# A list scheduler's table of durations: new figures for all engines, short strided copies, powers, selects and function table changes

## The chip, the cores and the metric

The kernel runs on one core of one Trainium2 chip. The metric is the device time of one execution in microseconds. The core's engines each work through a queue of their own and meet at semaphores: TensorE (PE in the profile; its weight loads are PEld), VectorE (DVE), ScalarE (ACT), GpSimd (POOL) and SyncE (SP), which here does nothing but issue all the DMAs.

## The reference

One encoder block on 1024 tokens by 1024 features, all in float32. Cut to what is computed:

```
h = rms_norm(x, g_mix);  proj = h @ w_in        # 8224 columns: glu a, b | q k v | z | logits | gates A, B
c = silu(layer_norm(depthwise_conv31(glu_a * sigmoid(glu_b))));  y_conv = c @ w_conv_out
q, k, v = silu(depthwise_conv5(q, k, v));  q, k = l2_norm(q), l2_norm(k)
o = gated_delta_rule(q, k, v, g, beta) + reversed(gated_delta_rule(reversed ...))   # 8 heads of 128
y_delta = (rms_norm(o) * silu(z)) @ w_delta_out
x = x + (sigmoid(gate_a) * y_conv + sigmoid(gate_b) * y_delta) @ w_o
x = x + (silu(gt) * up) @ w_down                 # gt, up = rms_norm(x) @ w_gate_up, 2816 columns each
x = x + sigmoid(rms_norm(x) @ w_pl_gate) * rms_norm(p @ w_pl_proj)
out = rms_norm(x)
```

The gated delta rule is a recurrence over chunks of tokens. In each chunk a triangular system is solved, and a 128x128 state goes from chunk to chunk, in both directions.

## The kernel before

**What is computed in which form.** Activations stand as [feature, token]. A dense product multiplies 128 columns of a weight with 512 tokens; operands are split into a high and a low part of a reduced float32 type (`split`: a cast on ACT and a subtraction on DVE), and three matmuls of 128x512 make one product block (`mm3`). In the profile these are the rows `ps<-big,w`. The delta rule works in plain float32 with matmuls of 128x128; each of those leaves two records in the profile, so eight records are four matmuls.

**The stages.** Part 1 begins with the start: eight loads of x, RMSNorm, transposes on PE with `ident`, x itself transposed and stored (`d<-mid`), and the taps of the convolutions (`in_qkv_conv_w`, `in_conv_dw_w`). Then come the input projections (`qkv`, `glu`, `z`, `gate`), the convolutions on DVE, the projection of the per-layer embedding (`pl`), the convolution's LayerNorm (`ln`) and projection (`cout`), and beside them the delta rule, in four groups of two heads. Part 3 is dense products throughout: delta's projection, the output projection, SwiGLU up and down, the per-layer embedding's gate, and the output.

**A head of the delta rule**, by the sections named in the code: `d.np` makes the matrices from q and k. `d.inv` inverts 32x32 diagonal blocks on DVE. `d.lev` puts them together to 128x128 inverses, twice for four chunks each: sixteen copies of 32 partitions on ACT bring the blocks to their places (`eu`, `et`: rows `COPY big<-big 32x4x32`, 32x128 in the profile), a product on PE, its negation on ACT (`m<-ps`), a second product, four more copies and two small transposes on DVE, then a third product, a negation, a fourth product and two copies. `d.chain` runs through the chunks, both directions in turn; each step is a product, a combination on DVE or ACT, and the next product (tiles `S`, `xin`, `z`). `d.out` adds the products within the chunks (matmuls `ps<-big,m`; two selects on POOL make the masks), takes squares with a sum on ACT (`m,sso<-big`), raises them to the power -1/2 on POOL (`rn`), multiplies on DVE (`m<-big,rn`) and transposes on PE (`ps<-ident,m`).

**What sets the order.** The block is first written down as a list of instructions on stand-ins for tiles (`add` and what calls it). `Plan.order` then gives them an order by list scheduling: each engine takes, at the time at which it comes free in the plan, the instruction of the lowest level that is ready by then; levels (`LV`) put weights first (-3.0), then the delta rule (-1.8), with the dense products behind (0.5 to 2.7). An instruction is ready when what it reads has ended in the plan, plus a latency by the two engines (`LAT`), and when its tiles have a free buffer. `HOLD` lets DVE wait up to 0.24 us for something more urgent; ACT passes over an instruction that needs another function table up to `AGE` = 4 times. The durations in the plan are the costs that `matmul`, `transpose`, `act`, `_vec`, `square_transpose`, `recip`, `pow`, `fill` and `select` write down, and `SWITCH` for a change of ACT's table; DMAs take `DMA_LAT` and a rate. The plan's times are used for nothing but the order: on the chip each engine runs its queue in that order, and the waits are real ones.

Of the kernel before, what the change touches and what calls it, by code (L numbers as in the profile page):

```python
# ---------------------------------------------------------------- the order of the instructions
# The block is first written down as a list of instructions on stand-ins for tiles. `Plan.run` gives
# them an order by list scheduling (which engine does what when, with what each instruction waits for
# and how many buffers there are) and then issues them in that order, on tiles made as they come up.
# [12 lines left out]
ALU = mybir.AluOpType  # L17
# [19 lines left out]
class Buf:  # L37
    """A stand-in for a tile."""
# [15 lines left out]
class View:  # L54
    """Part of a tile: partitions [p0, p1), free dimensions as (stride, size) from an offset."""
# [40 lines left out]
    def fold(self, *sizes):  # L96
        """The last free dimension cut into dimensions of these sizes."""
        s, n = self.dims[-1]
        dims = []
        for k in reversed(sizes):  # L100
            dims.append((s, k))
            s *= k
        return View(self.buf, self.p0, self.p1, self.off, self.dims[:-1] + dims[::-1], self.cast)
# [4 lines left out]
    def spread(self, *shape):  # L108
        """Dimensions of size one repeated to these sizes."""
# [28 lines left out]
class Op:  # L138
    """An instruction: its engine, how to issue it, and what it reads and writes."""


# functions that need a table of their own in ScalarE, and the price of a change of tables
TABLES = {AF.Exp: 0, AF.Sigmoid: 1, AF.Silu: 2, AF.Ln: 3}
SWITCH = 2.0
AGE = 4
# a DMA: from its issue to its data, and bytes in a microsecond
# [3 lines left out]
# from the end of an instruction to the start of one that needs it, by the engines of both  # L150
# [7 lines left out]
class VPool:  # L158
# [5 lines left out]
    def tile(self, shape, dtype=F32, tag=None, bufs=None, line=None, cap=99, stream=None):  # L164
        """line: tiles of a line are given out in the order of the program, at most cap at a time."""
# [7 lines left out]
class Plan:  # L173
# [11 lines left out]
    # -- recording  # L185
# [44 lines left out]
    # -- engines  # L230
    def matmul(self, out, lhsT, rhs, start, stop):
        n = rhs.n
        if rhs.buf.dtype == F32R and rhs.cast is None:
            cost = max(0.107, n / 2400 + 0.003)
        else:
            cost = 2 * max(0.107, n / 1200)
# [4 lines left out]
    def transpose(self, out, in_, ident):  # L241
        self.add("pe", lambda: self.nc.tensor.transpose(out.ap(), in_.ap(), ident.ap()), [out], [in_, ident], 0.107)  # L242

    def act(self, out, in_, func=AF.Copy, scale=1.0, bias=None, accum=None):
# [8 lines left out]
        if accum is not None:  # L253
            outs.append(accum)
            cost += 0.1
# [46 lines left out]
    def square_transpose(self, out, in_):  # L302
        self._vec("transpose", "dve", dict(out=out, in_=in_))

# [4 lines left out]
    def pow(self, out, in0, in1):  # L309
        self.add("pool", lambda: self.nc.gpsimd.tensor_tensor(out=out.ap(), in0=in0.ap(), in1=in1.ap(), op=ALU.pow),  # L310
                 [out], [in0, in1], 0.3 + out.n * 0.165)
# [5 lines left out]
    def select(self, out, in_, pattern, base, mult, op, fill=0.0):  # L317
        self.add("pool", lambda: self.nc.gpsimd.affine_select(
            out=out.ap(), in_=in_.ap(), pattern=pattern, base=base, channel_multiplier=mult, compare_op=op, fill=fill),
            [out], [in_], 0.14 + out.n * 0.00084)  # L320
# [13 lines left out]
    # -- scheduling  # L334
    def order(self):
# [6 lines left out]
        free_slots = {}     # (pool, tag) -> times at which slots come free  # L342
        queue = {}          # line -> tiles in program order
# [8 lines left out]
        wait = {e: [] for e in engs}       # heap by ready time: dependencies all scheduled  # L352
        avail = {e: [] for e in engs}      # heap by key: ready at the engine's time
# [6 lines left out]
        held = []                            # of a later phase  # L360
        last_end = {}
        parked = {}                          # (pool, tag) -> ops that wait for a slot
# [10 lines left out]
        def slots_ready(o, now):  # L373
            """None when it can go now; else (time or None, (pool, tag))."""
# [20 lines left out]
        while len(done) < total:  # L395
# [43 lines left out]
            # worth the wait: something more urgent is about to be ready  # L439
# [14 lines left out]
            o.start = now  # L454
            if o.table is not None and o.table != table:
# [46 lines left out]
    # -- issue  # L502
# [28 lines left out]
P = 128  # L531
# [25 lines left out]
# slots of each kind of tile, and what goes before what  # L557
# [22 lines left out]
# products of part 1 in order (k, q, v, g: glu, z, l: logits, p: per-layer embedding; with the head or  # L580
# block), and those that fill in
# [6 lines left out]
def ORDER(f):  # L588
    """The block up to the delta rule's end, in the order in which it is written down."""
# [10 lines left out]
def hybrid_block(tc, x, p, g_mix, w_in, conv_dw_w, conv_dw_b,  # L600
# [7 lines left out]
    big = pn.pool("big", N_BIG)          # 1024 columns and the padding of a convolution  # L608
    mid = pn.pool("mid", N_MID)          # 512 columns
# [30 lines left out]
    # ---------------------------------------------------------------- constants  # L640
# [13 lines left out]
    m_le = tri("m_le", 1, -1, 0, ALU.is_ge)      # 1 where partition <= column  # L654
    m_ge = tri("m_ge", -1, 1, 0, ALU.is_ge)      # 1 where partition >= column
    m_lt = tri("m_lt", 1, -1, 0, ALU.is_gt)      # 1 where partition < column
    m_gt = tri("m_gt", -1, 1, 0, ALU.is_gt)      # 1 where partition > column
    ident2 = const("ident2", [64, 32])           # two identities of 32, one above the other
# [18 lines left out]
    # ---------------------------------------------------------------- dense products  # L677
    def split(hi, lo, src, scale=None):
        """src (float32) as the sum of two float32r parts."""
# [7 lines left out]
    def load_w(w, r0, nk, c0, cap=4, pool=None):  # L687
        """nk blocks of 128 rows of w, 128 columns, split: by four blocks."""
# [22 lines left out]
    def block_half(w, acts, h, nk):  # L711
        """128 columns of w against 512 tokens: a bank of [column, token]."""
# [18 lines left out]
    def rows(r, n):  # L731
        """[P, n] values by token as a bank whose rows all hold them along the free axis."""
# [1033 lines left out]
```

## Time and profile before

| | us |
|---|---|
| median of 3 runs | 2144.21 |
| lowest, highest run | 2142.52, 2147.73 |
| profiled execution, span from first to last instruction | 2144.9 |
| PE busy in it | 2094.7 |
| DVE busy | 1606.4 |
| ACT busy | 1089.8 |
| POOL busy | 129.5 |

The page gives the profiled execution's span; its own time is not given beside it, and the span lies between the lowest and the highest of the runs. In the profile, a group's row has its line, engine, operation, tiles, shapes and count, then busy time and the mean of one in ns, then the idle time of the engine just before such instructions and what ended it. In the timeline a row has its start, its length, and in brackets the idle time before it. L242 and L237 are the lines of the transpose and of the matmul, L259 and L266 those of ACT, L282 of DVE, L310, L314 and L318 of POOL, L330 of the DMAs.

### The profile page before, as it was taken

The page shows a single profiled execution, that of the slowest core. Times are in us where ns is not written, and L with a number is a line of the kernel's source. Part 1 is how long each engine was busy: PE and PEld are TensorE (multiplying, and loading weights), DVE is VectorE, ACT ScalarE, POOL GpSimd, SP SyncE. Part 2 cuts the span into 40 slices and gives each one's busy share as a digit, 9 for nine tenths or more (in the row PEclk, how much of TensorE's full clock was granted, in tenths as well). Part 3 has the DMA queues.
Part 4 walks back from the last instruction along what each step waited for, and adds up shares of the span by engine and source line. Part 5 has one row for each costly group of instructions (what it writes and reads, how often), then busy time and mean ns, then how long its engine had stood idle before and what let it go on. Part 6 is the DMA issues. An engine that isn't in the chain of part 4 may idle for free.

```text
span 2144.9 us, 29696 instructions
## 1 busy us (share of the span) xinstructions
PE 2094.7 (98%) x10434; PEld 1736.6 (81%) x10434; DVE 1606.4 (75%) x2621; ACT 1089.8 (51%) x2501; POOL 129.5 (6%) x203
## 2 busy tenths in 40 slices
PE   7999999999999999999999999999999999999998
PEld 5888788878888788878888888888888888888888
DVE  4488999977898989887687868786666667452676
ACT  6636656756656655767775435533323334121542
POOL 1000201110100111011100000000000000000000
PEclk9999999999999999999999999999999999999999
DMA  6233224522423422635468687432222227231253
GB/s 213 100 123 127 84 81 138 187 79 79 138 89 120 146 74 79 197 122 182 157 213 254 195 262 229 123 99 84 80 78 84 84 80 273 67 95 39 66 170 108
DMA packets 289077, 278.69 MB, mean 130 GB/s; under 512 B 17209, under 2 KB 217074, under 8 KB 288928
## 3 DMA queue, kind: packets, MB, share of 16 engines
q1 hardware_dynamic: 288928, 276.79, 40.3%
q8 instruction: 82, 1.34, 0.3%
q14 instruction: 67, 0.55, 0.1%
HBM read 198.02 MB, written 78.71 MB: 129 GB/s over the span
## 4 chain that ended last, share of the span: by engine, by line
PE 86%; ACT 7%; DVE 5%; issue 1%; DMA 1%; SPq 0%; POOL 0%; DVEq 0%; POOLq 0%; ACTq 0%
PE ps L237 84%; ACT big L259 4%; DVE big L282 3%; PE ps L242 2%; DVE mid L282 1%; ACT big L266 1%; ACT m L266 1%; DVE w L282 1%; ACT w L259 1%; DMA big<-in_x_dram 1%; DMA d<-mid 0%; ACT mid L266 0%; SPq L330 0%; ACT L266 0%; ACT mid L259 0%
## 5 line engine op out<-in xcount | busy, mean ns | idle before, releaser
L237 PE MATMUL ps<-big,w 128*128 128x512 f32 (+1 forms) x7524 | 1848.7, 399 | 0.9 <-ACT w L259 0.8
L237 PEld LDWEIGHTS ps<-big,w 128*128 128x128 f32 x7524 | 1383.4, 189 | 305.3 <-ACT w L259 1.2
L282 DVE SCALAR_TENSOR_TENSOR big<-big,cw 128x1024 f32<-128x1024 f32 x336 | 434.2, 1299 | 17.3 <-ACT big L266 12.3
L259 ACT CAST w<-raw 128x512 fp32r<-128x512 f32 (+2 forms) x340 | 198.3, 589 | 365.0 <-PE ps L237 288.4
L282 DVE TENSOR_TENSOR w<-raw,w 128x512 fp32r<-128x512 f32 (+2 forms) x340 | 221.6, 659 | 124.9 <-ACT w L259 119.3
L282 DVE TENSOR_TENSOR big<-ps,big 128x512 f32<-128x512 f32 (+1 forms) x132 | 89.9, 687 | 86.4 <-PE ps L237 76.2
L259 ACT CAST w<-mid 128x512 fp32r<-128x512 f32 x125 | 77.2, 621 | 149.5 <-PE ps L237 109.5
L282 DVE TENSOR_TENSOR w<-mid,w 128x512 fp32r<-128x512 f32 x125 | 85.9, 688 | 62.3 <-ACT w L259 61.6
L237 PEld LDWEIGHTS ps<-big 128*128 128x128 f32 x784 | 101.9, 195 | 16.1 <-issue 9.1
L237 PE MATMUL ps<-big 128*128 128x128 f32 (+1 forms) x784 | 107.2, 283 | 7.7 <-ACT big L259 5.1
L282 DVE TENSOR_TENSOR big<-big 128x512 fp32r<-128x512 f32 (+2 forms) x159 | 107.0, 707 | 8.7 <-ACT big L259 8.4
L259 ACT COPY big<-big 32x128 f32<-32x128 f32 (+1 forms) x264 | 102.5, 440 | 16.5 <-DVE big L282 12.5
L259 ACT COPY big<-ps 32x128 f32<-32x128 f32 (+3 forms) x162 | 66.8, 413 | 64.3 <-PE ps L237 55.0
L259 ACT CAST big<-big 128x512 fp32r<-128x512 f32 x120 | 69.9, 619 | 42.5 <-DVE big L282 21.3
L242 PE MATMUL ps<-ident,big 128*128 128x128 f32 (+1 forms) x432 | 72.0, 280 | 13.6 <-DMA big<-in_x_dram 9.3
L237 PEld LDWEIGHTS ps<-S,big 128*128 128x128 f32 x448 | 71.8, 190 | 10.0 <-DVE S L282 0.2
L237 PE MATMUL ps<-S,big 128*128 128x128 f32 x448 | 75.0, 275 | 0.0
L242 PEld LDWEIGHTS ps<-ident,big 128*128 128x128 f32 (+1 forms) x432 | 53.9, 147 | 25.2 <-issue 13.4
L237 PEld LDWEIGHTS ps<-big,m 128*128 128x128 f32 x512 | 64.1, 195 | 12.2 <-ACT m L266 9.4
L237 PE MATMUL ps<-big,m 128*128 128x128 f32 x512 | 66.1, 280 | 6.4 <-ACT m L266 6.3
L266 ACT ACTIVATE mid<-mid 128x512 f32<-128x512 f32 (+2 forms) x87 | 50.2, 580 | 38.6 <-DVE mid L282 26.8
L266 ACT ACTIVATE big<-big 128x1024 f32<-128x1024 f32 (+2 forms) x80 | 56.6, 715 | 22.2 <-DVE big L282 17.2
(158 smaller groups left out, 1711.0 us busy)
## 6 DMA issues: line engine op xcount, KB each, us to landing
d<-mid SPq DMA_DIRECT2D x162, 256.0 KB, 3.0
raw<-in_w_in_dram SPq DMA_DIRECT2D x128, 256.0 KB, 3.0
mid<-d SPq DMA_DIRECT2D x120, 256.0 KB, 3.4
big<-d SPq DMA_DIRECT2D x92, 256.0 KB, 4.0
big<-dqkv SPq DMA_DIRECT2D x32, 512.0 KB, 4.9
raw<-in_w_gate_up_dram SPq DMA_DIRECT2D x50, 256.0 KB, 2.9
dqkv<-big SPq DMA_DIRECT2D x24, 512.0 KB, 2.9
mid<-in_w_gate_up_dram SPq DMA_DIRECT2D x46, 256.0 KB, 4.0
```

The source lines that it names most:

```text
L237: o = self.add("pe", lambda: self.nc.tensor.matmul(out.ap(), lhsT.ap(), rhs.ap(), start=start, stop=stop), [out], [lhsT, rhs], cost)
L242: self.add("pe", lambda: self.nc.tensor.transpose(out.ap(), in_.ap(), ident.ap()), [out], [in_, ident], 0.107)
L259: return self.nc.scalar.copy(out.ap(), in_.ap())
L266: return self.nc.scalar.activation(out.ap(), in_.ap(), func, **kw)
L282: return getattr(e, name)(**{k: v.ap() if isinstance(v, View) else v for k, v in kw.items()})
```

## The change

The prices of the table are set anew, and matmuls and transposes count double while the plan's clock is under 25 us (`COLD`). Beside this the comments are gone, so the lines move by up to eight. Nothing else differs: the same instructions are written down, with the same levels, buffers and latencies.

```diff
-SWITCH = 2.0
+SWITCH = 1.31
 AGE = 4
+COLD = 25.0
...
         if rhs.buf.dtype == F32R and rhs.cast is None:
-            cost = max(0.107, n / 2400 + 0.003)
+            cost = max(0.111, n / 2208 + 0.0015)
         else:
-            cost = 2 * max(0.107, n / 1200)
+            cost = 2 * max(0.111, n / 1200)
...
         if accum is not None:
             outs.append(accum)
-            cost += 0.1
+            cost += 0.125 if in_.buf.pool.space == PSUM else 0.1
+        if out.p1 - out.p0 < P and out.buf.tag == "big" and out.n <= 256:
+            cost += 0.125
...
     def square_transpose(self, out, in_):
         self._vec("transpose", "dve", dict(out=out, in_=in_))
+        self.ops[-1].cost += 0.14
...
-                 [out], [in0, in1], 0.3 + out.n * 0.165)
+                 [out], [in0, in1], 0.85 + out.n * 0.09 if out.n != 1 else 1.48)
...
-            [out], [in_], 0.14 + out.n * 0.00084)
+            [out], [in_], 0.1 + out.n * 0.00165 if out.n > P else 0.25)
...
             o.start = now
+            if e == "pe" and now < COLD:
+                o.cost *= 2
```

The price of a transpose on PE goes from 0.107 to 0.110. By these rules a copy of 32 partitions and 128 elements within SBUF goes from 0.200 to 0.325 us, a matmul of 512 columns from 0.216 to 0.233. PE's queue is cut into 1218 rows of equal instructions instead of 1271, and ACT's queue holds 36 table loads instead of 42.

The order moves on every engine. Three places follow. The first is the end of head 0 (`d.out`) on ACT: `m,sso` are the squares, the copies of 32 partitions belong to the inverses of head 1. Before:

```order
L266 ACTIVATE big<-ps,bb 128x128
L259 COPY big<-big 32x4x32 x18
L266 ACTIVATE m_2345,sso<-big 128x128
L259 COPY big<-big 32x4x32
L266 ACTIVATE m_2345,sso<-big 128x128 x3
L259 COPY big<-big 32x4x32 x2
L266 ACTIVATE m_2389,sso<-big 128x128 x4
```

With the change:

```order
L263 CAST w<-raw 128x512
L263 COPY big<-big 32x4x32 x8
L270 ACTIVATE m_2297,sso<-big 128x128
L263 COPY big<-big 32x4x32
L270 ACTIVATE m_2297,sso<-big 128x128 x3
L263 COPY big<-big 32x4x32
L270 ACTIVATE m_2345,sso<-big 128x128 x4
```

Eight copies stand ahead of the first square instead of 18, one instead of two between the first four and the last four; the rest follow behind. On PE, at the same place, `ps<-big,m` are the last products of the delta rule, `ps<-ident,m` the transposes. Before:

```order
L237 MATMUL ps<-big,m_2347 128x128
L237 MATMUL ps<-big,w 128x512 x36
L242 MATMUL ps<-ident,m_2932 128x128 x4
L237 MATMUL ps<-big,w 128x512 x4
L242 MATMUL ps<-ident,m_2949 128x128 x4
```

With the change:

```order
L239 MATMUL ps<-big,m_2299 128x128
L239 MATMUL ps<-big,w 128x512 x25
L244 MATMUL ps<-ident,m_2789 128x128 x4
L244 MATMUL ps<-ident,m_2796 128x128 x4
L239 MATMUL ps<-big,w 128x512 x3
```

The transposes move up by eleven dense products, and the four products between their two halves go. The second place is the first half of the inverses of head 6 on PE, from its first product (`big 128x128`) over the second (`big,m`) and third to the fourth. Before:

```order
L237 MATMUL ps<-big 128x128 x4
L242 MATMUL ps<-ident,big 128x128 x4
L237 MATMUL ps<-big,w 128x512 x3
L237 MATMUL ps<-big,m_8997 128x128 x4
L242 MATMUL ps<-ident,big 128x128 x4
L237 MATMUL ps<-big,w 128x512 x5
L237 MATMUL ps<-big 128x128 x4
L237 MATMUL ps<-big,w 128x512 x2
L242 MATMUL ps<-ident,big 128x128 x4
L237 MATMUL ps<-big,w 128x512
L237 MATMUL ps<-big,m_9056 128x128 x4
```

With the change:

```order
L239 MATMUL ps<-big 128x128 x4
L239 MATMUL ps<-big,w 128x512
L239 MATMUL ps<-big,m_8897 128x128 x4
L239 MATMUL ps<-big 128x128 x4
L239 MATMUL ps<-big,w 128x512 x2
L239 MATMUL ps<-big,m_8936 128x128 x4
```

The transposes of the per-layer embedding (`ident,big`) have gone to head 7, and of the dense products between the steps 1, 0 and 2 are left. The third place is SP's queue in the start, from the fifth and sixth load of x on. Before:

```order
L330 DMA big<-in_x_dram 128x1024 x2
L330 DMA big<-in_qkv_conv_w_dram 5x1024 x2
L330 DMA d_205<-mid 128x512
L330 DMA d_216<-mid 128x512
L330 DMA d_227<-mid 128x512
L330 DMA big<-in_x_dram 128x1024 x2
L330 DMA d_252<-mid 128x512
L330 DMA raw<-in_w_in_dram 128x4x128 x2
```

With the change:

```order
L335 DMA big<-in_x_dram 128x1024 x2
L335 DMA big<-in_qkv_conv_w_dram 5x1024 x2
L335 DMA d_202<-mid 128x512
L335 DMA d_210<-mid 128x512
L335 DMA d_218<-mid 128x512
L335 DMA d_227<-mid 128x512
L335 DMA raw<-in_w_in_dram 128x4x128 x2
L335 DMA d_287<-mid 128x512
L335 DMA big<-in_x_dram 128x1024
L335 DMA d_302<-mid 128x512
L335 DMA d_313<-mid 128x512
L335 DMA raw<-in_w_in_dram 128x4x128
L335 DMA big<-in_x_dram 128x1024
```

The seventh load of x comes behind one more store, two weight loads and a fifth store; the eighth behind two more stores and a weight load. Further down, the load of the long convolution's taps has 8 of the 16 stores of x behind it instead of 6.

More of the change, by code (lines that the diff above doesn't have):

```diff
@@ L138 @@
 class Op:
+    pass
 TABLES = {AF.Exp: 0, AF.Sigmoid: 1, AF.Silu: 2, AF.Ln: 3}
-SWITCH = 2.0
+SWITCH = 1.31
 AGE = 4
+COLD = 25.0
 DMA_LAT, DMA_RATE = 1.6, 300000.0
@@ L241, in transpose @@
     def transpose(self, out, in_, ident):
-        self.add("pe", lambda: self.nc.tensor.transpose(out.ap(), in_.ap(), ident.ap()), [out], [in_, ident], 0.107)
+        self.add("pe", lambda: self.nc.tensor.transpose(out.ap(), in_.ap(), ident.ap()), [out], [in_, ident], 0.110)
     def act(self, out, in_, func=AF.Copy, scale=1.0, bias=None, accum=None):
```

## The prediction

> **What bounds the kernel now.** The first view is the page's head, then the busy times of TensorE (PE) by stage.
>
> ```profile
> span 2144.9 us, 29696 instructions
> PE 2094.7 (98%) x10434; PEld 1736.6 (81%) x10434; DVE 1606.4 (75%) x2621; ACT 1089.8 (51%) x2501; POOL 129.5 (6%) x203
> ...
> 0.00:60.00 60.00, 45.72 (x247) 0.91 0.58 190
> 60.00:225.00 165.00, 165.00 (x766) 1.00 0.36 119
> 225.00:1100.00 875.00, 848.79 (x4731) 0.99 0.39 124
> 1100.00:2085.00 985.00, 985.00 (x4274) 1.00 0.43 134
> 2085.00:2145.00 60.00, 50.16 (x425) 0.94 0.35 114
> ```
>
> PE is busy in 2094.7 of 2144.9 us. The columns of the five stages are length, PE's busy time with its matmuls, granted clock, DMA share and GB/s. From 1100 to 2085 us, nearly half of the span, PE has no gap and full clock: 985.00 us for 4274 matmuls is 0.2305 us apiece. No order can shorten that stage, nor the stretch from 60 to 225 us. A new order can only touch three things: 14.3 us without work in the first 60 us, 26.2 us between 225 and 1100 us (875 less 848.79), where the delta rule runs beside the dense products, and 9.8 us at the end.
>
> The next view is who PE waited for, over the whole span.
>
> ```profile
> PE ps L242 <- DVE m L282: 11.2, 5, 3.7
> PE ps L242 <- DMA big<-in_x_dram: 9.3, 3, 8.9
> PE ps L237 <- ACT m L266: 6.3, 5, 2.4
> PE ps L237 <- ACT big L259: 5.1, 3, 3.3
> ...
> PE ps L237 <- DVE big L282: 1.4, 2, 1.0
> PE ps L237 <- issue: 1.1, 1, 1.1
> ```
>
> Columns: us in total, times, longest. The first row is the end of a head (`d.out`): PE stands before the transposes of the normalised output. ACT m, ACT big, DVE big and issue, 13.9 us together, are the inverses (`d.lev`): PE waits for negated products (m) and for copied blocks (big). These 25.1 us are nearly all of the 26.2. The wait for x is the start.
>
> Third view: where the granted clock fell after such waits (same columns).
>
> ```profile
> 320.00:330.00 10.00, 6.73 (x30) 0.83 0.17 59
> 470.00:480.00 10.00, 6.91 (x30) 0.95 0.55 158
> 480.00:490.00 10.00, 9.82 (x43) 0.71 0.01 2
> 550.00:560.00 10.00, 6.79 (x31) 0.88 0.28 79
> 560.00:570.00 10.00, 9.87 (x60) 0.95 0.50 157
> 1020.00:1030.00 10.00, 5.83 (x33) 0.93 0.29 97
> 1030.00:1040.00 10.00, 10.00 (x62) 0.73 0.50 156
> ```
>
> Ten times one minus the clock, summed over the seven rows, is 1.7 + 0.5 + 2.9 + 1.2 + 0.5 + 0.7 + 2.7 = 10.2 us: lost time inside what counts as busy. So what an order can win between 225 and 1100 us is about 36 us, 1.7%.
>
> **The change, step by step.** Nothing is computed otherwise and no instruction gets faster; only the order on each queue moves. I compare each price with its row.
>
> ```profile
> L259 ACT COPY big<-big 32x128 f32<-32x128 f32 x256 | 93.9, 418 | 16.5 <-DVE big L282 12.5 <-POOL big L314 2.4 <-issue 0.2
> L266 ACT ACT_TABLE_LOAD x41 | 52.6, 1283 | 1.0 <-DVE big L282 0.3
> L318 POOL TENSOR_SCALAR_AFFINE_SELECT m<-m 128x512 f32<-128x512 f32 x32 | 35.5, 1111 | 156.7 <-DMA m<-d 85.5 <-PE ps L237 31.7 <-ACT z L266 29.3
> L310 POOL TENSOR_TENSOR rn<-rn,mhalf 128x8 f32<-128x8 f32 x8 | 17.9, 2238 | 108.6 <-DVE rn L282 108.6
> L310 POOL TENSOR_TENSOR fr<-fr,mhalf 128x1 f32<-128x1 f32 x8 | 5.3, 657 | 93.0 <-DVE fr L282 93.0
> ```
>
> The dense matmul was priced 0.216 and is now 0.233, beside 0.2305 measured. The 32-partition copy was 0.200 and is 0.325, beside 0.418 for one. A table change was 2.0 and is 1.31, beside 1.283. The select of 512 columns was 0.57 and is 0.945, beside 1.111. Two prices stay off: the power of 128x8 goes from 1.62 to 1.57 beside 2.238, and that of one column from 0.465 to 1.48 beside 0.657. VectorE's large operations keep their prices. So ACT and PE come right, and the powers do not.
>
> *Term 1, the end of a head.* The timeline of head 0 shows how the old prices made the wait.
>
> ```profile
> 311.94 6.02 ACT L259 COPY big<-big 32x128 f32<-32x128 f32 x16
> 314.24 8.65 PE L237 MATMUL ps<-big,w 128*128 128x512 f32 x36
> 317.86 0.30 ACT L266 ACTIVATE m<-big 128x128 f32<-128x128 f32 x1
> ...
> 321.16 0.29 ACT L266 ACTIVATE m<-big 128x128 f32<-128x128 f32 x1
> 322.03 2.60 POOL L310 TENSOR_TENSOR rn<-rn,mhalf 128x8 f32<-128x8 f32 x1 [6.70 <-DVE rn L282]
> 324.66 0.69 DVE L282 TENSOR_TENSOR m<-big,rn 128x512 f32<-128x512 f32 x1 [0.33 <-POOL rn L310]
> 325.41 1.11 PE L242 MATMUL ps<-ident,m 128*128 128x128 f32 x4 [2.52 <-DVE m L282]
> ```
>
> Sixteen copies for head 1 hold ACT for 6.02 us (0.376 each; the plan had 3.2 us) ahead of the eight squares; then come power, product and transpose. From the end of PE's delta products at 314.24 to the transpose at 325.41 are 11.2 us; 36 dense products cover 8.65 of them, and 2.52 stay as a wait. In the changed order 8 copies stand there instead of 18, and 25 dense products instead of 36. Ten copies fewer take 10 x 0.376 = 3.8 us out, so the need falls to 7.4; the cover falls by 11 x 0.2305 = 2.5 to 6.1, and 1.3 us of waiting are left. Counted over the eight heads, the cover falls from 246 to 218 dense products (by head 36, 28, 40, 31, 30, 30, 26, 25 before, and 25, 27, 30, 25, 30, 31, 24, 26 after), 6.5 us less; the copies ahead of the squares fall only in heads 0, 4 and 6 (18 to 8, 18 to 8, 12 to 8). Head 0 keeps 1.3 of 2.52, half of its wait; I let that share stand for the 11.2 and take 5.6 us left: **-5.6**. Bounds: all of it gone, -11.2; or the cover lost and the need not shorter, +6.5.
>
> *Term 2, the inverses.* With copies and PE priced as measured, the first product of an inverse is placed later beside its copies. But in head 6 the changed order has almost nothing to put between the steps: 1, 0 and 2 dense products, where 7, 9 and 7 small or dense ones stood. The row of before:
>
> ```profile
> 941.06 1.13 PE L237 MATMUL ps<-big 128*128 128x128 f32 x8 [1.25 <-ACT big L259]
> ...
> 944.39 1.16 PE L237 MATMUL ps<-big,m 128*128 128x128 f32 x8 [1.06 <-ACT m L266]
> ...
> 948.14 1.16 PE L237 MATMUL ps<-big 128*128 128x128 f32 x8 [0.99 <-DVE big L282]
> ```
>
> Here 3.3 us are waited with that cover: four transposes and 3, then 5 dense products, some 1.1 and 1.6 us. With 0.2 and 0 instead, 0.9 and 1.6 come on top, so 5.8 us for head 6. The other 10.6 of the 13.9 I take as reduced to 4, a judgement: copies remain priced 0.05 short and sixteen of them make 0.8 us a head. Together 9.8 for 13.9: **-4.1**, bounds -11 (only the bare 2.5 of head 6 left) and +2.5 (head 6 alone changes).
>
> *Term 3, the clock.* The drops stood behind waits of 2.4 to 3.3 us. If one drop like that of 470 to 490 us (0.5 + 2.9) is left, in head 6, 3.4 of the 10.2 us stay: **-6.8**, bounds -10.2 and +3.4 (one drop more).
>
> *Term 4, the chain of head 7.* The changed order sets the short products of the per-layer embedding beside head 7's chain and the gates later; some twenty steps of a chain, most of them there, have at most three dense products (0.7 us) between them, where six had so few before. PE waited for no `z`, `S` or `xin` in the rows above; if each of the fourteen more lacks one product of 0.2305 us, that is **+3**. Bounds 0 (other steps' slack takes it) and +10 (twenty steps, 0.5 each).
>
> *Term 5, the start.* The last two loads of x stand further back in SP's queue: the seventh behind four stores, two weight loads and another store, the eighth behind two more stores and a weight load. SP waits at each store for ACT's copy, so they leave some 6 us later. What ends the start, though, is another thing:
>
> ```profile
> 35.17 0.25 SPq L330 DMA_DIRECT2D big<-in_conv_dw_w_dram  x1
> 35.68 9.19 DMA d<-mid
> ```
>
> Stores behind the taps of the long convolution land 9.19 us later, and ACT's next copies need their buffers. That load comes earlier now relative to the work left, with 8 stores behind it instead of 6. Late x against earlier taps: **0**, bounds -4 and +5. The dearer matmul, and its doubling for the first 25 us of the plan, also put ten dense products (2.3 us) out of the start; they are inside these bounds.
>
> Part 3 and the end keep rows of the same kind without waits: 0, because PE there is at 985.00 of 985.00 us.
>
> The sum: -5.6 - 4.1 - 6.8 + 3 + 0 = -13.5, from 2144.9 to 2131.4. The profiled execution is 0.7 us above the median of the runs, 2144.21, so the forecast is 2130.7, said as **2131**. Its own range: every term halfway to its better bound gives 2120, and terms 1 and 5 halfway to their worse ones, the others kept, give 2140.
>
> **A rule against it.** The table change is the one price that falls far. Its row gives 1283 ns for a load, and nothing in this trace shows ACT held any longer behind one. The Trainium skill, page "ScalarE: Activation LUTs", section "What ACT_TABLE_LOAD costs", says that a drain of about 1.38 us comes on top, about 2.66 us for every switch. By that page the change moves the price away from the truth; what would follow is the fourth rival.
>
> **The rivals.**
>
> *The covers shrink, the needs do not* (slower). The old plan took PE for 6% faster than it is (0.216 for 0.2305), so PE came late to its appointments; that slack goes. VectorE's prices and the powers' stay too low, so its results may come as late as before. Price: term 1 at +6.5, one clock drop more at +3.4, terms 2 and 5 at zero, term 4 at +3: 2144.9 + 12.9 = 2157.8. For it speaks the power, 2.238 us against a price of 1.57; against it the copies that left ACT's queue, 3.8 us in head 0. It decides from where head 0's need stays above 8 us.
>
> *The starved places give it back* (no change). Term 1 at -5.6 as forecast, but in heads 6 and 7 PE runs dry: term 4 at +10, term 2 at 0, and half of the clock drops stay (-5.1): 2144.2. That the plan itself has no dense product ready in head 6 speaks for it.
>
> *All planned waits vanish* (faster). -11.2, -11 and -10.2 with nothing back: 2144.9 - 32.4 = 2112.5. Against it speak the two starved places.
>
> *Each table change is priced short.* If ACT stood as long again behind a load as the load itself takes, 1.283 us, and that hit one step of each of the eight heads for which PE waits, PE would lose 8 x 1.283 = 10.3 us: 2131.4 + 10.3 = 2141.7. The loads' row speaks against it.
>
> **How the numbers follow.** Chances: forecast 0.52, starved 0.22, slower 0.13, all gone 0.11, table change 0.02. Within 0.3% of the median (2137.8 to 2150.6) is what a measurement cannot tell from no change. Of the forecast's 0.52, some 0.05 lies above 2137.8. So faster has 0.47 + 0.11 = 0.58, same 0.05 + 0.22 + 0.02 = 0.29, slower 0.13. The range takes in the forecast, the starved case and most of "all gone", and leaves out the slower rival and the far end: 2113 to 2149.
>
> **What would show it.** Right: the wait for DVE m near 5 to 6 us, head 0's first transpose waiting under 2 us, fewer than seven windows under full clock, and a wait of 2 us or more between the steps of head 6's inverse. Wrong in term 1: DVE m at 11 us or more, with the squares still late on ACT. Wrong in term 4: head 7's chain without gaps, or with over 6 us of them. Wrong in term 5: the first 60 us with over 18 us or under 11 us without matmuls. Wrong altogether: any gap between 1100 and 2085 us.

## The result, and the profile after

The changed kernel takes **2154.92 us** (median of 4 runs, 2153.88 to 2155.1) against 2143.53 us before (4 runs, 2142.52 to 2147.73): a ratio of 1.0049, 95% interval 1.0035 to 1.0063. It is slower by 0.5%, where 0.6% faster had been forecast; the time lies 6 us above the range. The profiled execution took 2155.1 us, with a span of 2153.4, 8.5 us longer than the span before. The medians lie 11.4 us apart, not 8.5: in every run here the time is some 1.7 us more than the span, so the profiled execution before, with its span of 2144.9, took some 2146.6 us, 3.1 above its median. The prediction had set that span against the times.

The head of the page of the changed kernel, and PE's busy time by stage (length, PE busy with its matmuls, the same for weight loads, VectorE, ScalarE and GpSimd, then clock, DMA share, GB/s):

```profile
span 2153.4 us, 29679 instructions
PE 2102.0 (98%) x10434; PEld 1733.1 (80%) x10434; DVE 1602.6 (74%) x2621; ACT 1082.5 (50%) x2495; POOL 129.1 (6%) x203
```

```profile
0.00:60.00 60.00, 47.16 (x256) 36.02 (x257) 25.38 (x48) 39.95 (x68) 8.21 (x25) 0.94 0.60 190
60.00:225.00 165.00, 163.40 (x757) 132.52 (x756) 122.48 (x197) 83.80 (x189) 7.86 (x18) 1.00 0.36 115
225.00:1100.00 875.00, 854.23 (x4745) 719.64 (x4744) 756.17 (x1227) 585.59 (x1582) 103.88 (x149) 0.99 0.39 128
1100.00:2085.00 985.00, 979.13 (x4213) 788.55 (x4212) 650.32 (x1041) 349.35 (x598) 4.03 (x4) 0.99 0.41 130
2085.00:2155.00 70.00, 58.11 (x470) 56.40 (x468) 48.24 (x112) 23.78 (x59) 5.09 (x8) 0.95 0.37 116
```

The stretch in which the delta rule runs has 20.8 us without matmuls (875 less 854.23) instead of 26.2: the gain that was looked for is there. What is new is the fourth row: PE had 985.00 of 985.00 us there, and now stands for 5.87. This is the sign that the prediction named as "wrong altogether". (The second row, full before, now lacks 1.60 us, chiefly by one wait of 1.5 us at 223 us.) PE's waits over the span of the changed kernel (total us, times, longest):

```profile
PE ps L244 <- DMA big<-in_x_dram: 8.1, 4, 7.5
PE ps L239 <- ACT big L263: 6.2, 4, 2.6
PE ps L239 <- DVE w L286: 5.8, 3, 3.6
PE ps L239 <- ACT m L270: 4.4, 8, 1.4
...
PE ps L244 <- DVE m L286: 2.9, 5, 0.9
...
PE ps L239 <- DVE S L286: 1.7, 3, 1.3
...
PE ps L239 <- DVE big L286: 1.6, 2, 1.3
PE ps L239 <- DVE xin L286: 1.5, 2, 0.8
```

DVE m, the end of a head, is down from 11.2 to 2.9. ACT big, ACT m and DVE big, the inverses, are at 12.2 where they and "issue" were 13.9. S and xin, the chain, are new in the list, and so is DVE w: PE waits for weights that VectorE sums for the projection of the delta rule, the first product of part 3. The clock by windows of 10 us says the same (same columns as the stages):

```profile
320.00:330.00 10.00, 9.85 (x60) 8.35 (x60) 9.73 (x11) 8.22 (x22) 1.26 (x4) 1.00 0.45 149
480.00:490.00 10.00, 10.00 (x62) 8.61 (x61) 8.65 (x10) 8.50 (x22) 0.89 (x1) 1.00 0.56 179
...
920.00:930.00 10.00, 6.35 (x27) 5.20 (x27) 9.30 (x10) 9.49 (x28) 0.00 (x0) 0.63 0.00 0
930.00:940.00 10.00, 10.00 (x55) 8.87 (x55) 8.84 (x10) 4.08 (x11) 1.61 (x4) 0.86 0.59 211
...
1170.00:1180.00 10.00, 7.93 (x26) 5.38 (x26) 9.93 (x17) 5.78 (x10) 0.00 (x0) 0.83 0.14 47
1200.00:1210.00 10.00, 6.39 (x22) 4.79 (x21) 9.83 (x18) 3.69 (x7) 0.00 (x0) 0.79 0.35 119
1210.00:1220.00 10.00, 10.00 (x39) 8.00 (x38) 7.67 (x12) 3.66 (x7) 0.00 (x0) 0.87 0.93 303
```

The drops at 320 and 480 us are gone. Between 225 and 1100 us one is left, in head 6, with 10 x (0.37 + 0.14) = 5.1 us instead of 10.2. Two new ones lie at the entry of part 3, with 10 x (0.17 + 0.21 + 0.13) = 5.1 us. With the 5.87 us of waits the entry costs **11.0 us**, more than the whole growth of the span, 8.5 us.

How this happens is read from three queues of the changed kernel, around 1175 us. PE, VectorE and SP in turn (start, length, instruction; in brackets the wait before it):

```profile
1162.82 9.75 PE L239 MATMUL ps<-big,w 128*128 128x512 f32 x41
1173.97 0.73 PE L239 MATMUL ps<-big,w 128*128 128x512 f32 x2 [1.40 <-ACT w L263]
1175.37 16.66 PE L239 MATMUL ps<-big,w 128*128 128x512 f32 x63 [0.67 <-DVE w L286]
1192.23 11.45 PE L239 MATMUL ps<-big,w 128*128 128x512 f32 x48 [0.19 <-ACT w L263]
1207.29 9.01 PE L239 MATMUL ps<-big,w 128*128 128x512 f32 x27 [3.61 <-DVE w L286]
```

```profile
1166.86 4.84 DVE L286 TENSOR_TENSOR big<-big 128x512 f32<-128x512 f32 x7
...
1172.22 2.49 DVE L286 TENSOR_TENSOR big<-big 128x512 fp32r<-128x512 f32 x4
...
1180.05 1.27 DVE L286 TENSOR_TENSOR mid<-ps,mid 128x512 f32<-128x512 f32 x2
```

```profile
1180.76 0.93 SPq L335 DMA_DIRECT2D d<-mid  x2
1181.74 1.99 SPq L335 DMA_DIRECT2D big<-d  x4
```

The four `big<-d` loads bring the last pair of heads to part 3. In the code they wait for the 14th of the 16 stores of the convolution's projection (`OT_AFTER`, 13 counted from zero). That block's last product is the eighth of the 41 from 1162.82, so it ends at about 1162.82 + 8 x 0.234 = 1164.7. Its multiply (`mid<-ps,mid`) runs at 1180.05, **15 us** later: VectorE does sums of part 3 (`big<-big`, `w<-...`) in between, because part 3 has level 1 and the convolution's projection (`cout`) has 2.4, and the lower level goes first. So urgent work holds up the less urgent work that it waits for itself. Store, loads and sums follow, and PE waits 3.61 us for `w` at 1207. (The waits of 1.40 and 0.67 us come before that multiply: there PE's queue has products of part 3, whose weights are not split yet, ahead of the last ones of `cout`.) Before, the same multiply came soon, and its store and the load at once behind it:

```profile
1171.34 0.68 DVE L282 TENSOR_TENSOR mid<-ps,mid 128x512 f32<-128x512 f32 x1
```

```profile
1172.05 0.32 SPq L330 DMA_DIRECT2D d<-mid  x1
1172.42 0.43 SPq L330 DMA_DIRECT2D big<-d  x1
```

There the block's products had ended at 1168.0, 3.3 us ahead of the multiply.

### The profile page after: what moved, and what is told of

Read it like the earlier page. It is cut to its first block, busy times and chain, and to the rows that moved or that the text cites. A ratio compares the mean times of both kernels' runs of the same rounds, so it can differ in the third digit from the quotient of the medians.

```text
span 2153.4 us, 29679 instructions
## 1 busy us (share of the span) xinstructions
PE 2102.0 (98%) x10434; PEld 1733.1 (80%) x10434; DVE 1602.6 (74%) x2621; ACT 1082.5 (50%) x2495; POOL 129.1 (6%) x203
## 4 chain that ended last, share of the span: by engine, by line
PE 52%; DVE 3%; ACT 2%; issue 1%; DMA 0%; SPq 0%; DVEq 0%; POOLq 0%; POOL 0%; ACTq 0%
PE ps L239 52%; DVE big L286 2%; ACT big L263 1%; DVE mid L286 1%; DVE w L286 0%; PE ps L244 0%; DMA mid<-d 0%; ACT mid L270 0%; ACT big L270 0%; ACT m L270 0%; ACT mid L263 0%; ACT w L263 0%; SPq L335 0%; ACT z L270 0%; DVE lnb L286 0%
## 5 line engine op out<-in xcount | busy, mean ns | idle before, releaser
L286 DVE TENSOR_TENSOR big<-big 128x512 fp32r<-128x512 f32 (+2 forms) x159 | 107.4, 708 | 10.6 <-ACT big L263 10.2
L263 ACT COPY big<-big 32x128 f32<-32x128 f32 (+1 forms) x264 | 102.4, 441 | 15.5 <-DVE big L286 9.1
L263 ACT CAST big<-big 128x512 fp32r<-128x512 f32 x120 | 71.2, 619 | 44.3 <-DVE big L286 23.1
L244 PE MATMUL ps<-ident,big 128*128 128x128 f32 (+2 forms) x432 | 73.8, 286 | 10.4 <-DMA big<-in_x_dram 8.1
L244 PEld LDWEIGHTS ps<-ident,big 128*128 128x128 f32 (+2 forms) x432 | 55.1, 149 | 22.7 <-issue 10.5
```

What stands on the lines that cost most here:

```text
L263: return self.nc.scalar.copy(out.ap(), in_.ap())
L286: return getattr(e, name)(**{k: v.ap() if isinstance(v, View) else v for k, v in kw.items()})
```

## The experiments

Medians of several runs each; "before" ran beside them with 2143.55, 2144.02 and 2143.87 us in the three series.

**1. The convolution's projection first.** On the changed kernel:

```diff
-LV = dict(w=-3.0, logits=-0.2, delta=-1.8, qkv=1.3, glu=1.2, z=0.5, conv31=2.7, gate=2.3, pl=-0.3, ln=2.1, cout=2.4)
+LV = dict(w=-3.0, logits=-0.2, delta=-1.8, qkv=1.3, glu=1.2, z=0.5, conv31=2.7, gate=2.3, pl=-0.3, ln=2.1, cout=0.9)
```

> The changed kernel, with the level of the convolution's output projection put ahead of the delta projection's (cout 0.9 in place of 2.4; dout stays at 1). Theory: what was lost at the entry of part 3 (from 3.3 us ahead of before in the last products of cout to 7.6 us behind it at the first product of wo) comes from the order there: products and sums of dout go ahead of the last products and multiplies of cout, although the last loads of dout wait for cout's stores. Then PE's waits for DVE w between 1160 and 1215 us go (5.8 us over the span in the changed kernel), the two half-clock windows at 1175 and 1205 us go, and the time is 2144 (2142 to 2147), against 2154.9 of the changed kernel. Rival A: VectorE is the bound there whatever the order; the waits move to 1190 to 1230 us and the time stays at 2151 to 2156. Rival B: the loss is in the delta rule's stretch and only shows at this place; the time stays within 3 us of 2155.

Measured: 2143.03 us, ratio to before 0.9997 (0.9988 to 1.0007). The stage after 1100 us has no gap:

```profile
1100.00:2085.00 985.00, 985.00 (x4286) 796.09 (x4286) 659.65 (x1060) 356.21 (x615) 4.68 (x5) 1.00 0.42 133
```

The theory holds: 11.9 us come back by this one priority. It also tells what the new table was worth ahead of the entry: nothing that can be measured, since this kernel takes as long as the one before, whose entry has no wait either.

**2. TensorE's prices alone**, on the kernel before:

```diff
-            cost = max(0.107, n / 2400 + 0.003)
+            cost = max(0.111, n / 2208 + 0.0015)
...
-            cost = 2 * max(0.107, n / 1200)
+            cost = 2 * max(0.111, n / 1200)
...
-        self.add("pe", lambda: self.nc.tensor.transpose(out.ap(), in_.ap(), ident.ap()), [out], [in_, ident], 0.107)
+        self.add("pe", lambda: self.nc.tensor.transpose(out.ap(), in_.ap(), ident.ap()), [out], [in_, ident], 0.110)
```

> The kernel before, with TensorE's three prices alone changed as in the change (512 columns 0.216 to 0.233, the floor 0.107 to 0.111, the transpose 0.107 to 0.110). Theory: any change of the plan loses the order that the kernel before has at the entry of part 3; its loss of about 11 us shows here too, with the wait for DVE w at 4 to 8 us and half clock between 1160 and 1230 us: 2150 to 2160. Rival (the covers shrink because PE is no longer taken for faster than it is): the loss is in the delta rule, with PE's wait for DVE m at 11 us or more and more than five half-clock windows before 1100 us, and no waits after 1100 us; also 2150 to 2160, so the place decides, not the time.

Measured: 2183.33 us, 1.0188 (1.0173 to 1.0203), far over both. PE's waits:

```profile
PE ps L242 <- DVE m L282: 17.9, 5, 4.7
PE ps L237 <- ACT big L259: 13.3, 4, 4.2
...
PE ps L237 <- DVE w L282: 4.8, 4, 3.6
```

By the waits, theory and rival are both there: the entry's wait (DVE w), and above all the prediction's slower rival. The likely reading is that PE priced as slow as it is, with the copies still at 0.200, gives each need too few dense products: DVE m goes from 11.2 to 17.9 us, ACT big from 5.1 to 13.3.

**3. The power's price alone**, on the kernel before:

```diff
-                 [out], [in0, in1], 0.3 + out.n * 0.165)
+                 [out], [in0, in1], 0.85 + out.n * 0.09 if out.n != 1 else 1.48)
```

> The kernel before, with the price of the power alone changed as in the change (8 columns 1.62 to 1.57, 4 columns 0.96 to 1.21, one column 0.465 to 1.48): 28 of 15,000 instructions, none of them at the entry of part 3. Theory: the entry is a matter of chance in the plan, so this small change is enough to lose the order there: waits after 1100 us of 5 us or more, 2149 to 2157. Rival (a truer price for PE is what harms): PE's price is the old one here, so the entry stays without a wait and the time is 2143.5, within 4 us.

Measured: 2147.36 us, 1.0016 (1.0007 to 1.0026). The time is just inside the rival's 4 us, and below the theory's range; the waits tell more. The stage after 1100 us has 4.5 us without matmuls, and a wait for DVE w is in the list:

```profile
1100.00:2085.00 985.00, 980.50 (x4235) 788.92 (x4234) 664.63 (x1063) 365.58 (x623) 4.03 (x4) 1.00 0.42 133
```

```profile
PE ps L237 <- DVE w L282: 4.2, 4, 1.4
```

The theory had put these waits at 5 us or more, the rival at none. So a price that no instruction at the entry carries was enough to lose its order, in part.

**4. The change without the price of the short copies:**

```diff
-        if out.p1 - out.p0 < P and out.buf.tag == "big" and out.n <= 256:
-            cost += 0.125
```

> The changed kernel without the price of the short strided copies (0.325 back to 0.200). The entry of part 3 has the same order as in the changed kernel, so the loss there stays at about 11 us. Theory 1 (the truer price of the copies is what shortened the end of a head, 11.2 to 2.9 us waiting for DVE m): without it the wait for DVE m is back at 7 to 12 us, and the time is 2158 to 2165. Theory 2 (waits at the inverses and at a head's end are set by what the plan happens to have as filling, not by this price): the waits of the inverses, 16 us in the changed kernel, and those for DVE m move by up to 5 us either way, and the time is 2148 to 2158.

Measured: 2179.67 us, 1.0166 (1.0151 to 1.0181), above both.

```profile
PE ps L239 <- ACT big L261: 17.0, 4, 4.9
PE ps L244 <- DVE m L284: 14.6, 5, 4.1
```

Theory 1 holds and was put too small: this price is worth 24.8 us in the change (2179.67 less 2154.92), as much at the inverses (ACT big 6.2 to 17.0) as at the heads' ends (2.9 to 14.6).

**5. The dense product at 0.230, the powers as measured, and cout first.** On the kernel of run 1:

```diff
-            cost = max(0.111, n / 2208 + 0.0015)
+            cost = max(0.111, n / 2208 - 0.002)
...
-                 [out], [in0, in1], 0.85 + out.n * 0.09 if out.n != 1 else 1.48)
+                 [out], [in0, in1], (2.24 if out.n == 8 else 1.6) if out.n != 1 else 0.66)
```

> The changed kernel with conv's output projection first (as in the run before), the dense product of 512 columns at 0.230 (0.2305 measured, 0.233 in the change), and the power as measured: 2.24 for 8 columns, 1.6 for 4, 0.66 for one. Theory (with the entry mended, what is left is the few prices still off; a table that agrees with the trace lets the plan see every wait and fill it): the waits of the inverses fall from 16 to under 6 us, DVE m from 2.9 to under 2, the half clock at 923 to 934 us goes: 2127 to 2135. Rival (the waits of heads 6 and 7 come from work running out there, whatever the prices): they stay or move, 2139 to 2147.

The expectation takes 0.2305 us for the measured price of a dense product, and so do those of runs 10 to 12. It is not: 985.00 us for 4274 matmuls counts the smaller ones too, 106 of them. A long row of dense products alone, from the kernel before, says more:

```profile
1355.75 144.53 PE L237 MATMUL ps<-big,w 128*128 128x512 f32 x618
```

Less the 0.40 us of the last one, that is 144.13 us for 617 steps, 0.2336 each. So the 0.2334 of the change was the measured price, and 0.230 is 1.6% too cheap.

Measured: **2126.25 us**, 0.9918 (0.9899 to 0.9936), the fastest. Between 225 and 1100 us the clock is full and 14.75 us are without matmuls:

```profile
225.00:1100.00 875.00, 860.25 (x4809) 729.03 (x4808) 763.88 (x1235) 593.48 (x1590) 114.39 (x151) 1.00 0.40 131
```

```profile
PE ps L239 <- ACT m L270: 3.9, 4, 1.3
...
PE ps L239 <- ACT big L263: 3.4, 3, 1.4
...
PE ps L244 <- DVE m L286: 1.7, 3, 1.0
```

The time is just under the theory's, and the half clock is gone; the waits of the inverses fell less than it said, for ACT m and ACT big from 10.6 to 7.3 us. The reason that it gives, a table that agrees with the trace, does not hold, since the price of the dense product left the trace here. (The 16 us of the expectations counted a second row of ACT big, 3.7 us, that belongs to other products.)

**6. The control: cout first on the kernel before**, the edit of run 1 alone.

> The kernel before, with conv's output projection put first (cout 0.9), no price changed: the control for the first run. Theory (cout first only mends an entry that the plan has got wrong; the one before has no wait there): no gain, 2141 to 2150. Rival (cout first is worth 10 us by itself, and the changed kernel's entry was no worse than that of before): 2131 to 2136.

Measured: 2154.43 us, 1.005 (1.0032 to 1.0068). No gain, as the theory says, but a loss beyond it: PE now comes to this projection early and waits 7.0 us between 1100 and 1200 us (ACT big 3.7, DVE big 3.3), and the clock falls behind that. The new priority mends one wrong order; it is not good by itself.

**7. The copies' price alone**, on the kernel before (the two lines of run 4 added).

> The kernel before, with the price of the short strided copies alone (0.200 to 0.325). Theory (the old prices of PE and of the copies were both too low, and their errors cancelled; either alone upsets the balance): the delta rule's waits for DVE m and for the inverses fall from 25 to under 18 us, since the plan now puts more dense products over the copies, but PE runs out of filling sooner and waits elsewhere, at the end of the delta rule and the entry of part 3: 2150 to 2175. Rival (the copies' price is good by itself): 2130 to 2142.

Measured: 2170.46 us, 1.0125 (1.0107 to 1.0143). One wait stands out in PE's timeline:

```profile
965.12 0.99 PE L237 MATMUL ps<-ones,big 128*128 128x1 f32 x4 [17.52 <-DVE big L285]
```

DVE m is at 6.6 instead of 11.2 us, ACT big at 2.7 instead of 5.1; but PE stands for 17.52 us before the sums of the convolution's LayerNorm, for which VectorE is still at the long convolution, and the products that are left come behind these sums in PE's queue. The time is the theory's, and DVE w at the entry has 5.0 us; the long wait lies in the middle of head 6's inverses, not at the delta rule's end.

**8. All of the change but PE's prices**, the edit of run 2 taken back on the changed kernel.

> The changed kernel with TensorE's three prices back as before: all of the change but PE. With the kernel before, the run with PE's prices alone (2183) and the changed kernel (2155) this makes a square. If the parts simply added, this would be 2143.5 + 2154.9 - 2183.3 = 2115. Theory (they don't add: PE's price and the others' are only worth something together): the needs are priced right and PE as too fast, so the plan puts too many dense products over each need; little waiting in the delta rule, under 15 us for DVE m and the inverses together, and the entry of part 3 still costs 5 to 10 us: 2143 to 2155. Rival (PE's truer price is what harms in the change): 2115 to 2135.

Measured: 2133.44 us, 0.9954 (0.994 to 0.9968): faster than before by 0.46%. Neither simply adding (2115) nor the theory's 2143 to 2155, but inside the rival's bounds: PE's truer price is what harms most in this change. With PE old, the other prices take the time from 2143.5 to 2133.4; with PE new, from 2183.3 to 2154.9. So PE's price costs 39.8 us beside the old ones and 21.5 beside the new.

**9. Run 5 without the power's prices.**

> The fastest run so far (2126) with the power's price back to that of the change (1.57, 1.21, 1.48): what is left of the 16.8 us that it gained on the run with cout first alone (2143.0) belongs to the dense product at 0.230. Theory (the power ends before each head's transposes, so its 0.7 us for 8 columns are worth a wait at each head): 2129 to 2136, with DVE m at 2 to 5 us. Rival (the power is too rare to matter): 2124 to 2128.

Measured: 2129.83 us, 0.9937 (0.9922 to 0.9952). The power is worth 3.6 us. Run 11 moves as much by another small step, but the place agrees: DVE m is at 3.9 us against 1.7, and over all runs with the new price of the copies beside a dense product at 0.230 or more it is at 2.9 to 4.0 without the measured powers and at 1.7 to 2.0 with them (changed, runs 1, 9, 12 against 5, 10, 11). The other 13.2 of run 5's 16.8 are the dense product at 0.230 in place of 0.233.

**10. Run 5 without cout first:** only the table of run 5.

> The fastest run so far (2126) without cout first: the level is that of the kernel before, so only the table is left, every price as measured. Theory (the order at the entry of part 3 has nothing to do with the truth of the table: the greedy plan loses there whatever the prices): 8 to 12 us slower than 2126, 2134 to 2138, with DVE w at 4 to 7 us and half clock between 1140 and 1210 us. Rival (a true table mends the entry also): 2124 to 2129.

Measured: 2136.6 us, 0.9962 (0.995 to 0.9974), 10.4 us above run 5.

```profile
PE ps L239 <- DVE w L286: 4.3, 2, 3.6
```

The theory holds in this: the table does not mend the entry, neither this one nor that of the change, in which the dense product was right.

**11. The dense product at 0.2305 instead of 0.2299**, else run 5 (`n / 2208 - 0.0014`).

> The fastest run so far with the dense product at 0.2305 in place of 0.2299, both within 0.3% of what the trace shows. If truth of the price were what decides, nothing moves: 2124 to 2129. If the order at single places is a matter of chance, a change of 0.3% in one price moves the waits of the inverses by some us: 2128 to 2140, with up to 5 us more for ACT big and ACT m.

Measured: 2129.99 us, 0.9939 (0.9923 to 0.9954). A change of 0.3% in one price moves 3.7 us. Both values lie under the 0.2336 of the trace, so truth does not tell them apart; counted from start to start (as explained after the experiments) 3.8 us more are lost at the inverses, 2.2 of them in head 7. From one such pair it can't be said how much of the time is a matter of chance in the order, but differences of this size should not be read as the worth of a price.

**12. The change with the dense product at 0.230** (`n / 2208 - 0.002`), nothing else.

> The changed kernel with one number altered: the dense product of 512 columns at 0.230 in place of 0.233. The table of the change is 1.3% above the measured 0.2305, which makes the plan give each need one to two dense products too few per hundred. Theory: this alone wins part of what lies between the change and the fastest run; the entry of part 3 stays bad: 2140 to 2150. Rival (1.3% are too little to matter): 2152 to 2157.

Measured: 2143.31 us, 0.9999 (0.9989 to 1.0008). That one number, 1.6% below the measured 0.2336, is worth 11.6 us. DVE w is still there with 5.2 us: the entry stays bad. With run 8 (in which the floor and the transpose have their old prices too), the time of the change rises with the price of the dense product: 2133.4 us at 0.216, 2143.3 at 0.230 and 2154.9 at 0.233. Runs 2, 9 and 11 move the same way. In each of these tables the price that is nearest to the trace is the slowest, and too cheap a cover did less harm than one priced as it is.

## Why the prediction was wrong, step by step

The waits alone do not add up: PE's idle time fell between 225 and 1100 us by 5.4 us and the loss of clock by 5.1, and yet run 1, which only lacks the bad entry, is no faster than before. The reason is how busy time is counted. A dense product lasts about 0.40 us in the profile, which models the ends of matmuls, but the next starts 0.234 us after it, so a stall of less than some 0.16 us leaves no gap. So I count from start to start: for each pair of neighbouring matmuls on PE the time between their starts, less the middle value for pairs of these kinds, summed where it exceeds 0.03 us. Each place includes the half clock that falls on it:

| place (us lost) | before | changed | run 1 | run 5 |
|---|---|---|---|---|
| start, to 62 us | 13.5 | 14.0 | 14.4 | 15.2 |
| inverses | 21.7 | 23.1 | 23.6 | 14.2 |
| end of a head | 13.9 | 5.5 | 5.5 | 2.9 |
| chain | 6.6 | 12.3 | 12.4 | 12.3 |
| dense products and all else beside the delta rule | 35.7 | 32.4 | 32.0 | 29.2 |
| entry and rest of part 3 | 0.7 | 11.7 | 0.9 | 1.4 |
| end | 3.0 | 3.4 | 2.9 | 2.4 |
| sum | 95.1 | 102.4 | 91.5 | 77.5 |

The sums move by +7.3, -3.6 and -17.6 us against the spans' +8.5, -2.5 and -19.0. Between the changed kernel and run 1 no place but the entry moves by more than 0.5 us.

**Term 1, the end of a head: right, and too small.** Forecast -5.6, waits for DVE m 11.2 to 2.9, so -8.3. Head 0 went as worked out: 25 dense products, and a transpose that waits 0.46 us, where 1.3 had been left.

```profile
297.85 6.09 PE L239 MATMUL ps<-big,w 128*128 128x512 f32 x25
304.40 1.26 PE L244 MATMUL ps<-ident,m 128*128 128x128 f32 x8 [0.46 <-DVE m L286]
```

Not all of it is the copies' doing. Head 2 went from 3.21 to 0.94 us, though its copies were not among those that fell; before, its multiply on VectorE stood behind the sum of a weight that waited 1.73 us for ScalarE, and that order is gone.

**Term 2, the inverses: wrong.** Forecast -4.1; by the waits -1.7, and start to start +1.4. Head 6 is as foreseen, 4.5 us against 5.8:

```profile
921.69 1.27 PE L239 MATMUL ps<-big 128*128 128x128 f32 x8 [2.54 <-ACT big L263]
922.61 0.77 PE L239 MATMUL ps<-big,w 128*128 128x512 f32 x1
924.00 2.07 PE L239 MATMUL ps<-big,m 128*128 128x128 f32 x8 [0.61 <-ACT m L270]
927.42 2.07 PE L239 MATMUL ps<-big 128*128 128x128 f32 x8 [1.35 <-DVE big L286]
```

The step that failed is "the other 10.6 of the 13.9 I take as reduced to 4, a judgement": in those rows the other heads still wait 7.7 us (12.2 less 4.5), and the stalls too short for a row, which the term left out, grew. At full clock the stalls before the inverses' products went from 29 to 51, together from 11.9 to 17.1 us. Behind the judgement stood "with copies and PE priced as measured, the first product of an inverse is placed later". The price of PE did come out as measured, and runs 2, 8, 9 and 12 show that this is what costs. With the dense product at 0.230 (run 12) the inverses lose 14.4 us instead of 23.1; 6.3 of these 8.7 us are in head 6, where 46 other matmul records stand between the inverses' 64 instead of 24 (44 before). With 0.216 (run 8) the stalls at full clock are 27, with 8.9 us, though head 6 runs dry there too. A likely reason is that a price of PE that is too low puts more dense products over each need than the plan thinks necessary, a margin for all that it prices too low elsewhere; the changed table took this margin away. Which of the other prices and latencies needed it is not shown.

**Term 3, the clock: right until 1100 us.** -5.1 for a forecast of -6.8: the one drop left was in head 6, as said, with 5.1 instead of 3.4 us. The 5.1 us of new drops at the entry were in no term.

**Term 4, the chain: right, and too small.** +3 forecast, most of it in head 7; waits of 3.6 us for S and xin are new, and start to start it is +5.7, of which head 7 has 3.6 (1.0 to 4.6). In run 5 head 7 is back at 1.2, but the chain's sum is 12.3 there too, spread over the other heads. Run 8, with PE's old price, has only some 2 us more than before: here too PE's price is what costs.

**Term 5, the start: 0 forecast, +0.5 measured**, within its bounds.

**Part 3: the step that decided.** "Part 3 and the end keep rows of the same kind without waits: 0, because PE there is at 985.00 of 985.00 us." It cost 11.0 us. Full rows before show only that the old order fed PE there. The change reordered VectorE's and SP's queues at the entry also, and the loads there wait for stores of the work ahead; the forecast looked at neither. Runs 1 and 10 show the cause (11.9 and 10.4 us by one priority); runs 2, 3, 4, 7 and 12 have the wait for DVE w with quite different prices, and run 8 one for ACT w instead. Why the old table hit an order without it is not settled beyond this: the power's price alone loses part of it.

**"ACT and PE come right, and the powers do not" / "VectorE's prices and the powers' stay too low": half wrong.** I compared prices with the time of one instruction, and PE's with a mean that counts smaller matmuls: "985.00 us for 4274 matmuls is 0.2305 us apiece" is short of the 0.2336 of a dense product, and the old price lay 7% under it, not 6%. The plan's prices are from start to start: in the changed kernel a short copy that follows another starts 0.333 us after it (middle value) beside a price of 0.325, though one lasts 0.418; VectorE's 512 columns at 0.60 to 0.61 beside 0.601, though one lasts some 0.68. VectorE had been right all along. The copies are nearly right by the middle value, but some follow after 0.43 us, and over the row of sixteen in the prediction they are 0.05 short, as it says. The powers were wrong, and cost 3.6 us in run 9.

**The rivals.** *The covers shrink* gave 2157.8, near the measured time, but by luck: the 11.0 us of the entry are not in its sum, and its sign, DVE m above 11 us, is not in the changed kernel. Its mechanism is real all the same: "PE came late to its appointments; that slack goes" is what runs 2, 8 and 12 show of PE's price, and at the ends of the heads the copies' price in the same change held it down (24.8 us, run 4). *The starved places give it back* is true of head 6 and of head 7's chain. *All planned waits vanish* is out, with 20.8 us left without matmuls between 225 and 1100 us. *Each table change is priced short* is out: of the 36 loads of the changed kernel, 34 start within 0.03 us of the end of what ran before them, each lasts 1.283 us, and behind 30 of them the next instruction starts within 0.03 us. The Trainium skill, page "ScalarE: Activation LUTs", section "What ACT_TABLE_LOAD costs", adds a drain of about 1.38 us; this trace does not show it.

## What to carry to other kernels

A stage without waits is no proof that a new order cannot hurt it: look at its first instructions on every queue, above all at loads that wait for stores of the work before, and at priorities that let work overtake what it waits for. Prices in a list scheduler only work against each other: the same true price of TensorE cost 40 us beside the old prices and 21 beside the other new ones, and 1.6% less than the truth for the engine that covers the others' latency won 12 us. An old price that is wrong may be a margin; ask what it covered before it is set right. Price what the next instruction sees, from start to start and for one shape alone, and read short stalls that way too, since busy time hides those that are shorter than the overlap.

## What the runs showed of the hardware

The clock drops came in steps: in all these kernels a drop between 60 us and the last matmuls costs 1.7, 3.4, 5.1, 6.8 or 10.2 us: multiples of 1.7, that is of 3.4 us at half speed. The Trainium skill, page "TensorE: Matmul & The Clock Gate", section "What's actually happening", has windows of about 3.4 us that run freely, which agrees: in the kernels before and changed and in runs 2 and 4 the drops also start whole multiples of 3.41 us apart. Its table "Why this matters for your kernels" wants no idle gap above some 3 us; here waits of 1.40 and 0.67 us within 3 us of each other, with 0.73 us of work between, were enough for a drop at 1175 us. In head 6 a drop began behind a wait of 2.54 us, and lasted 10.2 us over two more waits. On the other side a single wait of 3.71 us (791 us, before) and one of 2.60 us (467 us, changed) led to none. So the length of one gap does not decide here, and several short waits close together can cost clock as well as a long one does.
